# Feed-forward with one 512-column product per weight tile, whole banks, kept hidden units, scaled operands, and another planner clock

## The chip, the cores and the metric

The kernel runs on 1 core of one Trainium2 chip. The metric is the device time of one execution in microseconds (us), median of several runs. The engines of the core are TensorE (PE, matrix products into PSUM; its weight loads are listed apart as PEld), VectorE (DVE), ScalarE (ACT), GpSimd (POOL) and SyncE (SP, which issues most DMAs). PSUM has eight banks; one bank holds 128 partitions x 512 float32.

## The reference

One sequence of 256 tokens, width 1024, goes through a gated recurrent layer, a feed-forward, stick-breaking attention, a second feed-forward, and a second block (a block attention and a chunked recurrence side by side, merged). The change is about the two feed-forwards:

```python
def rms_norm(x, g):
    xf = x.astype(jnp.float32)
    y = xf * lax.rsqrt(jnp.mean(xf * xf, axis=-1, keepdims=True) + RMS_EPS)
    return (y * g.astype(jnp.float32)).astype(x.dtype)

def swiglu_ffn(x, w_in, w_out):          # D_FF = 2816
    gu = jnp.einsum("bsd,df->bsf", x, w_in)
    h = jax.nn.silu(gu[..., :D_FF]) * gu[..., D_FF:]
    return jnp.einsum("bsf,fd->bsd", h, w_out)
...
    h = h + swiglu_ffn(rms_norm(h, ffn_norm[layer]), ffn_w_in[layer], ffn_w_out[layer])
```

## The kernel before, in words

Activations stand with channels on partitions and the 256 tokens as columns; the residual stream is `h`, [128, 8, 256]. All weights, 2128 tiles of 128x128, come in the order of their use in pieces of 8 tiles (`raw`). A float32 product is made of float32r products: `prep` splits each weight into a rounded part `wh` (ACT or DVE, whichever is less behind, `round`) and the rest `wl` (DVE), and `split` does the same to an operand (`hi`, `lo`; tiles xh and xl for a normed `h`, hx for the gated hidden units). `gemm` (L479) multiplies one weight tile by a 256-column operand in three products, wh x hi, wh x lo, wl x hi, into one half `sl` of a bank. `gemm_t` (L491) is the form with the operand standing and 512 weight columns moving.

`Run` writes the program of all engines in one order. It keeps a clock for each engine: `mm` (L275) adds n/2400 + 0.0025 us for a float32r product of n columns to `pe_t`. Work on DVE and ACT that follows a product is a generator (a chain), polled after each weight tile by `tick` and taken a step further when its operands are due by those clocks; `prep_ahead` splits weights ahead, at most `wcap` pieces. `bank` (L296) hands out PSUM banks, four under the tag "acc" and four under "g"; each is a tile [128, 512] of its own, and `free` gives it back. The framework derives the semaphore waits from the reads and writes of tiles.

`ffn` (L982) has 22 pairs of columns j (gate and up, 16 weight tiles each, two halves of one bank). `gu_chain` multiplies the bank by the norm's factor `S` (one 128x512 DVE operation that also empties the bank), applies silu, multiplies, splits into hx. From j = 4 on each j is followed by one K chunk of ff_out (8 weight tiles into four "acc" banks, two outputs m in each); the last `LAST` = 5 chunks come by `project` (L963) and `tail`, bank after bank, and `resid_chain` adds a whole bank to `h`, which starts the next norm.

Other users of the banks, named in the text below by the tile that they fill: z and ge (recurrent layer's projections), ig (its gates, with rg on ACT), qk, vt (attention), fb, qb, aq, ag, bg, ak, gate (second block's projections), mg (merge), ple and o_ (its end), S and v8 (norm rows and a small transposition), ol (attention's output).

Of the kernel before, what the change touches and what calls it, by code (L numbers as in the profile page):

```python
# [11 lines left out]
F32 = mybir.dt.float32  # L12
# [15 lines left out]
# from blocks of this many tokens on, the scores are computed block by block  # L28
# [5 lines left out]
# the order of the recurrent layer's products; 1: in float32, without a split  # L34
# [11 lines left out]
# the order of the second block's projections  # L46
# [113 lines left out]
# the functions that share a table of the scalar engine  # L160
# [15 lines left out]
class Bank:  # L176
    def __init__(self, t, tag):
        self.t, self.tag, self.fresh = t, tag, True
# [5 lines left out]

class Run:
    """Emits the program in one order for all engines. Chains of vector and scalar work are
    generators; each is taken a step further, between matrix products, about when its operands
    are due, so that no engine's queue waits on another's for long."""
# [7 lines left out]
    def __init__(self, nc, tc, ctx, io):  # L196
# [14 lines left out]
        self.bank_live = {"acc": 0, "g": 0}  # L211
        self.bank_free = {"acc": [0.0] * 4, "g": [0.0] * 4}
# [4 lines left out]
    # -- engines, with the time each is thought to be done --  # L217
# [69 lines left out]
    BIG_BUFS = 46  # L287
# [7 lines left out]

    def bank(self, tag):  # L296
        while self.bank_live[tag] >= 4:
            self.advance("bank " + tag)
        self.bank_live[tag] += 1
# [4 lines left out]
        self.n += 1  # L304
        return Bank(self.ps.tile([128, 512], F32, name=f"{tag}_{self.n}", tag=tag, bufs=4), tag)

    def free(self, b, t):
        self.bank_live[b.tag] -= 1
        self.bank_free[b.tag].append(t)

    # -- the chains --
# [5 lines left out]
    def _ready(self, w):  # L317
        if isinstance(w, Fut):
            return self._ready(w.t) if w.t is not None else None
        if isinstance(w, Avail):  # L320
            f = sorted(self.bank_free[w.tag])
            return f[w.n - 1] if len(f) >= w.n else None
# [28 lines left out]
    def advance(self, why):  # L351
        """Nothing to do but to wait for the next step of a chain."""
# [22 lines left out]
    # -- the weights: loaded in the order of their use, split into two parts that sum to them --  # L375
# [54 lines left out]
    def gemm32(self, bank, sl, name, k, m, x, stop):  # L430
        """The same product in float32, which needs no split of the weights."""
# [47 lines left out]
    def gemm(self, bank, sl, name, k, m, x, stop):  # L479
        """One 128 x 128 tile of weights times a [128, 256] operand, to bank[:, sl]."""  # L480
# [9 lines left out]

    def gemm_t(self, banks, name, k, m, x, stop):  # L491
        """The same with the operand standing: tokens by four tiles of outputs."""
# [9 lines left out]
    def round(self, out, a):  # L502
        """To float32r, on the engine that is less behind."""
# [6 lines left out]
    def split(self, src, hi, lo):  # L510
        """hi + lo = src, each exact in float32r; a step of a chain."""
# [5 lines left out]
    # -- reciprocal roots of [128, n] columns, in float32 --  # L517
# [11 lines left out]
    def row(self, out, col):  # L529
        """out[p, t] = col[t, p]: columns of tokens to rows, the columns given for each p."""  # L530
        self.mm(out, col, self.ident, True, True)


def build(r):
# [27 lines left out]
    # ones multiplied until the first data are there: the tensor engine's clock is gated until it has worked  # L562
# [29 lines left out]
    class Norm:  # L592
        def __init__(self, gain, extra=None, first=False):
            """gain: columns; extra: columns of a second gain, with a norm between the two; first: for an
            operand in float32 as well, which is there sooner."""
# [6 lines left out]
            self.hi = [r.big("xh", dt=F32R) for _ in range(2)]  # L602
            self.lo = [r.big("xl", dt=F32R) for _ in range(2)]
            for i in range(8):
                self.x[i].hi = self.hi[i // 4][:, i % 4]
                self.x[i].lo = self.lo[i // 4][:, i % 4]
            for x in self.x:
                x.whole = Fut()

        def pair(self, p, src, dep):  # L610
            """The chain from two chunks of the residual stream to two operands."""
# [88 lines left out]
    def root(out, sums, n, done=None):  # L700
        """One over the root of sums / n + EPS, over [128, 256]."""
# [10 lines left out]
        # a step of Newton's: exp and ln alone leave more than float32's rounding  # L712
# [13 lines left out]
    def tail(banks, name, ks, xs, on_bank, ahead=1):  # L726
        """The last K chunks of a product, bank after bank, so that its results come one after another."""
# [74 lines left out]
    # ================= the recurrent layer =================  # L802
# [160 lines left out]
    def project(name, xs, nk, bias, next_gain, extra=None, accs=None, lead=0, ahead=1):  # L963
        """The rest of a product whose result joins the residual stream, and the norm behind it."""
# [16 lines left out]
    # ================= gated feed-forward =================  # L981
    def ffn(layer, norm, next_gain, extra=None):  # L982
        r.spawn(norm.stats(r.bank("acc"), str(layer) in WIDE))
        hx = [Fut() for _ in range(NJ)]

        def gu_chain(j, bank):
# [8 lines left out]
            o = r.big("hx", [128, 2, 256], F32R)  # L995
            hx[j].hi, hx[j].lo = o[:, 0], o[:, 1]
# [3 lines left out]
        nin, nout = f"ff_in{layer}", f"ff_out{layer}"  # L1000
        bs = [r.bank("g"), r.bank("g")]
# [4 lines left out]
        for j in range(2):  # L1006
            r.spawn(gu_chain(j, bs[j]))
        accs = None
        for j in range(2, NJ):
            b = r.bank("g")  # L1010
            for k in range(8):
                for c in range(2):
                    r.gemm(b, c, nin, k, j + c * NJ, norm.x[k], k == 7)
            r.spawn(gu_chain(j, b))
            kk = j - (LAST - 1)
            if j == 3:
                r.CALM, r.wcap = FFN_CALM, FFN_CAP
            if j == NJ - 1:
                r.CALM, r.wcap = Run.CALM, Run.wcap
            if 0 <= kk < NJ - LAST:  # L1020
                if accs is None:
                    accs = [r.bank("acc") for _ in range(4)]
                for m in range(8):
                    r.gemm(accs[m // 2], m % 2, nout, kk, m, hx[kk], False)
        return project(nout, hx, NJ, None, next_gain, extra, accs, NJ - LAST)

# [679 lines left out]
```

## Time and profile before

| | us |
|---|---|
| median of 3 runs | 838.8 (838.66 to 838.92) |
| span of the profiled execution | 837.3 |
| PE busy in it | 830.4 (99%) |
| DVE busy | 639.1 (76%) |
| ACT busy | 415.6 (50%) |
| feed-forward stages in it, about | 97 to 293 and 390 to 592 |

The profiled execution shows its span from the first to the last instruction; the median of the runs is 1.5 us above that. PE's records overlap, so how far apart products run is read from the starts in its timeline and not from the length of a record. A number in brackets behind a row is the time that the engine stood idle before it and what released it. A group's mean is the length of one record of that shape.

### The profile page before, as it was taken

Reading aid. Unit: us, or ns where it says so; the run is one execution under the profiler, and the core shown is the slowest. Engines: PE = TensorE matmul, PEld = TensorE weight load, DVE = VectorE, ACT = ScalarE, POOL = GpSimd, SP = SyncE. Lnnn points to the kernel's source line nnn. Section 1 sums busy time; section 2 is a strip of 40 time slices with the busy share of each in tenths; the row PEclk is TensorE's granted clock in tenths of the full one; section 3 lists DMA queues with packets and bytes.
Section 4 is the critical chain, followed back from the end, with each engine's and each line's share of the span. In section 5 each row is a group of like instructions: output and inputs, shape, how many; then the busy total and the mean of one; then the engine's idle time right before and its main releaser. Section 6 shows DMA issues by size and latency. Waiting matters only on the chain.

```text
span 837.3 us, 16580 instructions
## 1 busy us (share of the span) xinstructions
PE 830.4 (99%) x6670; PEld 805.8 (96%) x6670; DVE 639.1 (76%) x1236; ACT 415.6 (50%) x821; POOL 24.2 (3%) x57
## 2 busy tenths in 40 slices
PE   8999999999999999999999999999999999999998
PEld 7999999999999998989999999999999899999997
DVE  5999887565665798989976665666799967896774
ACT  4597555454543325364654454543453525645451
POOL 2300000000000001010000000000100000000000
PEclk9999999999999999999999999999999999999999
DMA  8946556655565434455566565664534544546501
GB/s 334 363 138 218 169 188 202 201 183 193 181 203 160 166 93 153 121 168 172 177 202 196 183 200 180 205 194 153 164 101 134 175 146 125 166 138 208 196 26 51
DMA packets 40844, 144.98 MB, mean 173 GB/s; under 512 B 4568, under 2 KB 5616, under 8 KB 40768
## 3 DMA queue, kind: packets, MB, share of 16 engines
q1 hardware_dynamic: 40320, 142.53, 52.7%
q0 software_dynamic: 448, 1.40, 0.6%
q8 instruction: 52, 0.85, 0.4%
q14 instruction: 24, 0.20, 0.1%
HBM read 142.85 MB, written 1.06 MB: 172 GB/s over the span
## 4 chain that ended last, share of the span: by engine, by line
PE 99%; DMA 0%; DVE 0%; issue 0%; ACT 0%; POOLq 0%
PE acc L277 52%; PE g L277 45%; PE g L1099 1%; DMA prm<-in_params 0%; PE g L1437 0%; DVE o L233 0%; DVE qb L233 0%; ACT S L258 0%; ACT o L260 0%; DVE xf L242 0%; POOLq L1663 0%
## 5 line engine op out<-in xcount | busy, mean ns | idle before, releaser
L233 DVE TENSOR_TENSOR wl<-raw,wh 128x512 fp32r<-128x512 f32 x518 | 346.1, 689 | 22.9 <-ACT wh L258 14.4
L277 PE MATMUL g<-xh,wh 128*128 128x256 f32 x808 | 229.9, 284 | 0.0
L277 PE MATMUL g<-xh,wl 128*128 128x256 f32 x808 | 228.6, 283 | 0.0
L277 PE MATMUL g<-xl,wh 128*128 128x256 f32 x808 | 228.6, 283 | 0.0
L258 ACT ACTIVATE wh<-raw 128x512 fp32r<-128x512 f32 x387 | 216.2, 617 | 0.2 <-DMA raw<-in_weights 0.2
L277 PEld LDWEIGHTS g<-xh,wh 128*128 128x128 f32 x808 | 155.1, 192 | 0.8 <-issue 0.6
L277 PEld LDWEIGHTS g<-xl,wh 128*128 128x128 f32 x808 | 155.1, 192 | 0.2
L277 PEld LDWEIGHTS g<-xh,wl 128*128 128x128 f32 x808 | 155.1, 192 | 0.0
L277 PE MATMUL acc<-xh,wh 128*128 128x256 f32 x448 | 129.5, 289 | 0.4 <-DVE qb L233 0.4
L277 PE MATMUL acc<-hx,wh 128*128 128x256 f32 x704 | 128.3, 283 | 0.0
L277 PE MATMUL acc<-xl,wh 128*128 128x256 f32 x448 | 126.6, 283 | 0.0
L277 PE MATMUL acc<-xh,wl 128*128 128x256 f32 x448 | 126.6, 283 | 0.0
L277 PEld LDWEIGHTS acc<-hx,wh 128*128 128x128 f32 x704 | 109.8, 192 | 0.0
L233 DVE TENSOR_TENSOR gu<-g,S 128x512 f32<-128x512 f32 x44 | 30.2, 691 | 95.2 <-PE g L277 95.2
L277 PE MATMUL acc<-hx,wl 128*128 128x256 f32 x352 | 99.6, 283 | 0.0
L260 ACT ACTIVATE gu<-gu 128x256 f32<-128x256 f32 x44 | 18.4, 418 | 160.4 <-DVE gu L233 160.4
L277 PEld LDWEIGHTS acc<-xh,wh 128*128 128x128 f32 x448 | 85.7, 191 | 4.7 <-issue 4.0
L277 PEld LDWEIGHTS acc<-xl,wh 128*128 128x128 f32 x448 | 85.8, 192 | 0.1
L277 PEld LDWEIGHTS acc<-xh,wl 128*128 128x128 f32 x448 | 85.7, 191 | 0.0
L277 PEld LDWEIGHTS acc<-hx,wl 128*128 128x128 f32 x352 | 67.6, 192 | 0.0
L248 DVE CAST wh<-raw 128x512 fp32r<-128x512 f32 x131 | 55.6, 425 | 0.0
L258 ACT ACTIVATE xh<-h,prm 128x256 fp32r<-128x256 f32 x24 | 11.2, 500 | 22.5 <-DVE h L233 13.9
(290 smaller groups left out, 1229.8 us busy)
## 6 DMA issues: line engine op xcount, KB each, us to landing
raw<-in_weights SPq DMA_DIRECT2D x265, 512.0 KB, 3.7
toep<-vrev POOLq DMA_DIRECT2D x2, 512.0 KB, 5.7
h<-in_x SPq DMA_DIRECT2D x1, 512.0 KB, 6.8
raw<-in_weights SPq DMA_DIRECT2D x1, 384.0 KB, 4.4
past<-in_past SPq DMA_DIRECT2D x1, 384.0 KB, 5.5
h<-in_x SPq DMA_DIRECT2D x2, 128.0 KB, 3.4
h<-in_x SPq DMA_DIRECT2D x1, 256.0 KB, 5.3
pt<-in_p POOLq DMA_DIRECT2D x1, 256.0 KB, 5.7
```

Of the source, the lines that this page charges most:

```text
L233: self.nc.vector.tensor_tensor(out, a, b, op)
L248: self.nc.vector.tensor_copy(out, a)
L258: self.nc.scalar.activation(out, a, f, scale=scale, **kw)
L260: self.nc.scalar.activation(out, a, f, bias=bias, scale=scale, **kw)
L277: self.nc.tensor.matmul(out, l, r, start=start, stop=stop, skip_group_check=True)
L1099: nc.tensor.transpose(tb[a].t[:, b], m[:, a, b], r.ident)
```

## The change

The feed-forward's products change form. Operand parts hi and lo lie side by side (tiles xq, hx), and `gemm2` makes one 512-column product wh x [hi | lo] over a whole bank and one 256-column product wl x hi into its first half; the two halves of the bank are added when it is emptied. For ff_in, a column j takes both banks of a PSUM tile (`Pair`): ACT copies the low halves out and DVE adds them to the high halves. `Norm.scaled` makes operands that already hold the factor `S`; columns j whose scaled operands are not there yet by the planner's clock keep the old form (`plain`; j = 0 to 3 in both layers of the built program). ff_out comes after all of ff_in, output m by output m, 22 chunks deep, a bank for each m; `out_chain` adds the two halves to `h` in two DVE operations. All hx stay on chip. PSUM is now four tiles `pp0` to `pp3` of two banks each, handed out by number; that holds for all stages of the kernel. `mm` adds 0.0133 instead of 0.0025 us. `FFN_CAP` goes from 12 to 8. Comments go, too.

```diff
-FFN_CAP = 12
-LAST = 5
+FFN_CAP = 8
...
+class Pair:
+    def __init__(self, t, n):
+        self.n = n
+        self.banks = [Bank(t[:, i], None, 2 * n + i) for i in range(2)]
+        self.high, self.low = t[:, :, 0:256], t[:, :, 256:512]
...
-        self.bank_live = {"acc": 0, "g": 0}
-        self.bank_free = {"acc": [0.0] * 4, "g": [0.0] * 4}
+        self.pp = [self.ps.tile([128, 2, 512], F32, name=f"pp{i}", tag=f"pp{i}", bufs=1) for i in range(4)]
+        self.bank_free = {i: 0.0 for i in range(8)}
...
-            self.pe_t += max(n / 2400, m / 1200) + 0.0025 if l.dtype == F32R else 2 * max(n / 1200, m / 1200) + 0.005
+            self.pe_t += max(n / 2400, m / 1200) + 0.0133 if l.dtype == F32R else 2 * max(n / 1200, m / 1200) + 0.005
...
-    BIG_BUFS = 46
+    BIG_BUFS = 47
...
+    BANKS = {"acc": (0, 1, 2, 3), "g": (4, 5, 6, 7), "any": tuple(range(8))}
+
+    def frees(self, tag):
+        return [i for i in self.BANKS[tag] if i in self.bank_free]
+
     def bank(self, tag):
...
-        self.bank_free[tag].sort()
-        t = self.bank_free[tag].pop(0)
+        n = min(self.frees(tag), key=lambda i: (self.bank_free[i], i))
+        t = self.bank_free.pop(n)
...
-        return Bank(self.ps.tile([128, 512], F32, name=f"{tag}_{self.n}", tag=tag, bufs=4), tag)
+        return Bank(self.pp[n // 2][:, n % 2], tag, n)
+
+    def pair_bank(self):
...
+        n = min(both(), key=lambda i: (when(i), i))
+        self.wait_to(when(n), "pair of banks")
+        del self.bank_free[2 * n], self.bank_free[2 * n + 1]
+        return Pair(self.pp[n], n)
...
+    def gemm2(self, bank, name, k, m, x, stop):
...
+        self.need(x, f"{name} {k}")
+        wh, wl = self.weight(name, k, m)
+        self.mm(bank.t, wh, x.hl, bank.start(), False)
+        self.mm(bank.t[:, 0:256], wl, x.hi, False, stop)
+        self.tick()
...
+        def scaled(self, src):
...
+                    a = r.stt(f[:, c], src[:, 2 * p + c], self.gain[:, 2 * p + c:2 * p + c + 1], self.S, OP.mult, OP.mult)
+                yield a
+                a = yield from r.split(f, t[:, :, 0], t[:, :, 1])
+                self.y[2 * p].t = self.y[2 * p + 1].t = a
...
-            yield norm.s
+            if plain:
+                yield norm.s
             w = r.big("gu")
-            t = r.tt(w[:, 0:2], v2(bank), bc2(norm.S), OP.mult)
-            r.free(bank, t)
+            if plain:
+                t = r.tt(w[:, 0:2], v2(pair), bc2(norm.S), OP.mult)
+            else:
+                yield r.act(w[:, 2:4], pair.low, AF.Copy)
+                t = r.tt(w[:, 0:2], pair.high, w[:, 2:4], OP.add)
+            r.free(pair, t)
...
-            b = r.bank("g")
+            plain = not all(y.t is not None and y.t <= r.pe_t + 0.3 * k for k, y in enumerate(norm.y))
+            b = r.bank("any") if plain else r.pair_bank()
             for k in range(8):
                 for c in range(2):
-                    r.gemm(b, c, nin, k, j + c * NJ, norm.x[k], k == 7)
...
+                    if plain:
+                        r.gemm(b, c, nin, k, j + c * NJ, norm.x[k], k == 7)
+                    else:
+                        r.gemm2(b.banks[c], nin, k, j + c * NJ, norm.y[k], k == 7)
...
-        return project(nout, hx, NJ, None, next_gain, extra, accs, NJ - LAST)
...
+        def out_chain(m, bank):
+            yield r.pe_t + 0.2
+            yield r.tt(h[:, m], bank.t[:, 0:256], h[:, m], OP.add)
+            t = r.tt(h[:, m], bank.t[:, 256:512], h[:, m], OP.add)
+            r.free(bank, t)
+            done[m].t = t
+
+        for m in range(8):
+            b = r.bank("any")
+            for k in range(NJ):
+                r.gemm2(b, nout, k, m, hx[k], k == NJ - 1)
+            r.spawn(out_chain(m, b))
+        return nn
```

How the order of the built program changes, at two places. In the rows a matmul stands as result<-operands with the columns of its result; [waits X] names the engine's semaphore that it waits for.

PE in the end of the second ff_out before: the end of bank acc_681 (outputs 0 and 1), and the start of acc_683's last chunks.

```order
L277 MATMUL acc_682_5212<-hx_900_6976,wl_883_6837 128x256
L277 MATMUL acc_681_5211<-hx_912_7066,wh_887_6870 128x256 [waits DVE_49] x2
L277 MATMUL acc_681_5211<-hx_912_7066,wl_888_6871 128x256
L277 MATMUL acc_681_5211<-hx_912_7066,wh_887_6870 128x256 x2
L277 MATMUL acc_681_5211<-hx_912_7066,wl_888_6871 128x256
L277 MATMUL acc_683_5213<-hx_861_6656,wh_887_6870 128x256 x2
L277 MATMUL acc_683_5213<-hx_861_6656,wl_888_6871 128x256
```

DVE before at that place, where `h_66<-acc_...` is the residual add of a bank:

```order
L233 TENSOR_TENSOR wl_915_7089<-raw_892_6915,wh_914_7088 128x512 [waits DVE_49]
L233 TENSOR_TENSOR h_66<-acc_681_5211,h_66 128x512 [waits PE_49]
L237 SCALAR_TENSOR_TENSOR xl_909_7033<-h_66,der_103,xh_907_7031 128x256 [waits Activation_49] x2
L233 TENSOR_TENSOR h_66<-acc_682_5212,h_66 128x512 [waits PE_49]
L237 SCALAR_TENSOR_TENSOR xl_909_7033<-h_66,der_103,xh_907_7031 128x256 [waits Activation_49] x2
L233 TENSOR_TENSOR h_66<-acc_683_5213,h_66 128x512 [waits PE_49]
```

PE in the first ff_out after: the last chunk of output m = 0 (hx_303, in one bank of pp3) and the first chunks of m = 1 (hx_166, hx_171, hx_183, in the other bank of pp3; the rows name only the tile).

```order
L286 MATMUL pp3_66<-hx_303_2459,wl_310_2477 128x256
L286 MATMUL pp3_66<-hx_166_1455,wh_309_2476 128x512
L286 MATMUL pp3_66<-hx_166_1455,wl_310_2477 128x256
L286 MATMUL pp3_66<-hx_166_1455,wh_309_2476 128x512
L286 MATMUL pp3_66<-hx_166_1455,wl_310_2477 128x256
L286 MATMUL pp3_66<-hx_171_1483,wh_312_2500 128x512 [waits DVE_49]
L286 MATMUL pp3_66<-hx_171_1483,wl_313_2501 128x256
L286 MATMUL pp3_66<-hx_171_1483,wh_312_2500 128x512
L286 MATMUL pp3_66<-hx_171_1483,wl_313_2501 128x256
L286 MATMUL pp3_66<-hx_183_1575,wh_312_2500 128x512 [waits DVE_49]
L286 MATMUL pp3_66<-hx_183_1575,wl_313_2501 128x256
```

DVE after at that place:

```order
L242 TENSOR_TENSOR wl_316_2528<-raw_295_2400,wh_315_2527 128x512 [waits DMAHW5_49,Activation_49]
L242 TENSOR_TENSOR wl_316_2528<-raw_295_2400,wh_315_2527 128x512 [waits Activation_49]
L242 TENSOR_TENSOR h_70<-pp3_66,h_70 128x256 [waits PE_49]
L242 TENSOR_TENSOR wl_319_2551<-raw_299_2431,wh_318_2550 128x512 [waits DMAHW6_49,Activation_49]
L242 TENSOR_TENSOR h_70<-pp3_66,h_70 128x256 [waits DVE_49,PE_49]
L242 TENSOR_TENSOR wl_319_2551<-raw_299_2431,wh_318_2550 128x512 [waits Activation_49]
```

What moved: before, the bank that DVE empties is a tile of its own, and the rows of PE behind it (acc_683) carry no wait. After, the first add `h_70<-pp3_66` waits for the count that the product hx_166 with wl_310 brings, and the product hx_171 with wh_312 for that add; the second add waits for hx_171 with wl_313, and hx_183 with wh_312 for the second add.

The second place is in the second block's projections, the group ag: PE before, from the end of bank acc_1034 to the next bank of the same group.

```order
L277 MATMUL acc_1034_8047<-xh_908_7032,wl_1032_8035 128x256
L277 MATMUL acc_1034_8047<-xh_908_7032,wh_1031_8034 128x256
L277 MATMUL acc_1034_8047<-xl_910_7034,wh_1031_8034 128x256
L277 MATMUL acc_1034_8047<-xh_908_7032,wl_1032_8035 128x256
L277 MATMUL acc_1044_8137<-xh_907_7031,wh_1036_8070 128x256 [waits DVE_49]
L277 MATMUL acc_1044_8137<-xl_909_7033,wh_1036_8070 128x256
L277 MATMUL acc_1044_8137<-xh_907_7031,wl_1037_8071 128x256 [waits DVE_49]
```

DVE before, with the read of that bank, `ag`:

```order
L248 CAST wh_1041_8116<-raw_1021_7951 128x512
L233 TENSOR_TENSOR wl_1042_8117<-raw_1021_7951,wh_1041_8116 128x512 [waits DVE_49]
L237 SCALAR_TENSOR_TENSOR h_66<-h_66,prm_65,S_931_7331 128x256
L233 TENSOR_TENSOR ag_1033_8046<-acc_1034_8047,S_931_7331 128x512 [waits PE_49]
L237 SCALAR_TENSOR_TENSOR h_66<-h_66,prm_65,S_931_7331 128x256
```

PE after at that place (both banks of the group are now in pp0):

```order
L286 MATMUL pp0_63<-xq_700_5634,wh_871_7077 128x256
L286 MATMUL pp0_63<-xq_700_5634,wl_872_7078 128x256 [waits DVE_49]
L286 MATMUL pp0_63<-xq_700_5634,wh_871_7077 128x256 x2
L286 MATMUL pp0_63<-xq_700_5634,wl_872_7078 128x256
L286 MATMUL pp0_63<-xq_700_5634,wh_871_7077 128x256 [waits DVE_49]
L286 MATMUL pp0_63<-xq_700_5634,wh_871_7077 128x256
```

DVE after, with the same read:

```order
L257 CAST wh_877_7143<-raw_863_7015 128x512 [waits DMAHW1_49]
L242 TENSOR_TENSOR wl_878_7144<-raw_863_7015,wh_877_7143 128x512 [waits DVE_49]
L242 TENSOR_TENSOR ag_869_7054<-pp0_63,S_791_6346 128x512 [waits PE_49]
L242 TENSOR_TENSOR wl_878_7144<-raw_863_7015,wh_877_7143 128x512 [waits Activation_49]
L257 CAST wh_880_7173<-raw_866_7037 128x512 [waits DMAHW2_49]
```

What moved: the read of ag itself stands in its queue as before, but the row of PE behind the second weight tile of the next bank (xq_700 with wh_871, the last row but one) now waits for it; before, the rows of acc_1044 wait for their weights alone.

## Rows read from the trace of the kernel before

**Rows 1.** The page: span, busy time by engine, clock in 40 slices, chain by engine.
```profile
span 837.3 us, 16580 instructions
...
PE 830.4 (99%) x6670; PEld 805.8 (96%) x6670; DVE 639.1 (76%) x1236; ACT 415.6 (50%) x821; POOL 24.2 (3%) x57
...
PEclk9999999999999999999999999999999999999999
...
PE 99%; DMA 0%; DVE 0%; issue 0%; ACT 0%; POOLq 0%
```

**Rows 2.** Timeline of PE at 200 us: start us, us, engine line op out<-in xcount.
```profile
200.00 0.28 PE L277 MATMUL g<-xh,wh 128*128 128x256 f32 x1
200.12 0.28 PE L277 MATMUL g<-xl,wh 128*128 128x256 f32 x1
200.24 0.28 PE L277 MATMUL g<-xh,wl 128*128 128x256 f32 x1
200.36 0.28 PE L277 MATMUL g<-xh,wh 128*128 128x256 f32 x1
```

**Rows 3.** Timeline of PE, 744 to 755 us, the stage with the operand standing.
```profile
744.29 0.40 PE L277 MATMUL acc<-wh,xh 128*128 128x512 f32 x1
744.53 0.40 PE L277 MATMUL acc<-wh,xl 128*128 128x512 f32 x1
744.76 0.39 PE L277 MATMUL acc<-wl,xh 128*128 128x512 f32 x1
...
747.04 0.39 PE L277 MATMUL acc<-wh,xh 128*128 128x512 f32 x1
...
754.98 0.39 PE L277 MATMUL acc<-wl,xh 128*128 128x512 f32 x1
```

**Rows 4.** Timeline of all engines at 587 us, end of ff_out.
```profile
587.36 0.28 PE L277 MATMUL acc<-hx,wl 128*128 128x256 f32 x1
...
587.68 0.69 DVE L233 TENSOR_TENSOR h<-acc,h 128x512 f32<-128x512 f32 x1 [1.44 <-PE acc L277]
...
588.08 0.28 PE L277 MATMUL acc<-hx,wl 128*128 128x256 f32 x1
```

**Rows 5.** Timeline of all engines at 612 us, the second block's first products.
```profile
612.77 1.29 DVE L233 TENSOR_TENSOR qb<-acc,S 128x512 f32<-128x512 f32 x2 [1.47 <-ACT S L258]
...
612.89 0.28 PE L277 MATMUL acc<-xh,wl 128*128 128x256 f32 x1
...
613.61 0.36 PE L277 MATMUL acc<-xh,wh 128*128 128x256 f32 x1 [0.44 <-DVE qb L233]
...
613.80 0.28 PE L277 MATMUL acc<-xl,wh 128*128 128x256 f32 x1
```

**Rows 6.** Timeline of all engines at 5 us, the program's first operand.
```profile
5.29 0.35 DVE L242 TENSOR_SCALAR xf<-h,prm 128x256 f32<-128x256 f32 x1 [4.23 <-DMA prm<-in_params]
...
5.71 0.80 PE L277 MATMUL g<-xf,raw 128*128 128x256 f32 x1 [1.25 <-DVE xf L242]
```

**Rows 7.** Groups by line, shapes apart: count | busy, mean ns of one | idle before.
```profile
L233 DVE TENSOR_TENSOR wl<-raw,wh 128x512 fp32r<-128x512 f32 x518 | 346.1, 689 | 22.9 <-ACT wh L258 14.4 <-issue 0.9
...
L233 DVE TENSOR_TENSOR gu<-g,S 128x512 f32<-128x512 f32 x44 | 30.2, 691 | 95.2 <-PE g L277 95.2
...
L237 DVE SCALAR_TENSOR_TENSOR xl<-h,prm,xh 128x256 fp32r<-128x256 f32 x24 | 10.8, 479 | 1.2 <-ACT xh L258 1.2
...
L233 DVE TENSOR_TENSOR h<-acc,h 128x512 f32<-128x512 f32 x12 | 8.3, 690 | 7.7 <-PE acc L277 7.6
...
L233 DVE TENSOR_TENSOR ol<-g,oh 128x256 fp32r<-128x256 f32 x8 | 3.4, 420 | 1.0 <-ACT oh L258 1.0
...
L258 ACT ACTIVATE wh<-raw 128x512 fp32r<-128x512 f32 x387 | 216.2, 617 | 0.2 <-DMA raw<-in_weights 0.2
...
L260 ACT ACTIVATE ig<-acc,prm 128x256 f32<-128x256 f32 x8 | 3.4, 485 | 0.1
...
L258 ACT ACTIVATE ple<-acc 128x512 f32<-128x512 f32 x4 | 2.4, 598 | 2.0 <-PE acc L277 1.9
```

**Rows 8.** Busy time in three windows (core 0: us, PE, PEld, DVE, ACT, POOL).
```profile
200.00:210.00 10.00, 10.00 (x86) 10.00 (x85) 5.63 (x10) 3.94 (x8) 0.00 (x0) 1.00 0.56 186
400.00:410.00 10.00, 10.00 (x84) 9.95 (x83) 9.55 (x19) 5.11 (x12) 0.00 (x0) 1.00 0.58 183
...
620.00:630.00 10.00, 10.00 (x87) 10.00 (x86) 9.96 (x21) 4.48 (x8) 0.00 (x0) 1.00 0.40 119
```

More of the change, by code (lines that the diff above doesn't have):

```diff
@@ L294, in small, with both, when @@
         return self.sb.tile([128, n], F32, name=f"{name}_{self.n}", tag=f"small{n}", bufs=8 if n < 64 else 1)
+    BANKS = {"acc": (0, 1, 2, 3), "g": (4, 5, 6, 7), "any": tuple(range(8))}
+    def frees(self, tag):
+        return [i for i in self.BANKS[tag] if i in self.bank_free]
     def bank(self, tag):
-        while self.bank_live[tag] >= 4:
+        while not self.frees(tag):
             self.advance("bank " + tag)
-        self.bank_live[tag] += 1
-        self.bank_free[tag].sort()
-        t = self.bank_free[tag].pop(0)
+        n = min(self.frees(tag), key=lambda i: (self.bank_free[i], i))
+        t = self.bank_free.pop(n)
         if not self.in_task:
             self.wait_to(t, "bank " + tag)
-        self.n += 1
-        return Bank(self.ps.tile([128, 512], F32, name=f"{tag}_{self.n}", tag=tag, bufs=4), tag)
+        return Bank(self.pp[n // 2][:, n % 2], tag, n)
+    def pair_bank(self):
+        def both():
+            return [i for i in range(4) if 2 * i in self.bank_free and 2 * i + 1 in self.bank_free]
+        def when(i):
+            return max(self.bank_free[2 * i], self.bank_free[2 * i + 1])
+        while not both():
+            self.advance("pair of banks")
+        n = min(both(), key=lambda i: (when(i), i))
+        self.wait_to(when(n), "pair of banks")
+        del self.bank_free[2 * n], self.bank_free[2 * n + 1]
+        return Pair(self.pp[n], n)
     def free(self, b, t):
-        self.bank_live[b.tag] -= 1
-        self.bank_free[b.tag].append(t)
+        if isinstance(b, Pair):
+            self.bank_free[2 * b.n] = self.bank_free[2 * b.n + 1] = t
+        else:
+            self.bank_free[b.n] = t
     in_task = False
@@ L601, in __init__, with parts, chain @@
             self.q = None
[L602 to L606, printed above, removed]
+            self.parts(self.x)
             for x in self.x:
                 x.whole = Fut()
+        def parts(self, x):
+            for p in range(4):
+                t = r.big("xq", [128, 2, 2, 256], F32R)
+                for c in range(2):
+                    f = x[2 * p + c]
+                    f.hl, f.hi, f.lo = t[:, c].rearrange("p a b -> p (a b)"), t[:, c, 0], t[:, c, 1]
+        def scaled(self, src):
+            self.y = [Fut() for _ in range(8)]
+            def chain(p):
+                yield self.s
+                f = r.big("xs", [128, 2, 256])
+                t = r.big("xq", [128, 2, 2, 256], F32R)
+                for c in range(2):
+                    y = self.y[2 * p + c]
+                    y.hl, y.hi, y.lo = t[:, c].rearrange("p a b -> p (a b)"), t[:, c, 0], t[:, c, 1]
+                    a = r.stt(f[:, c], src[:, 2 * p + c], self.gain[:, 2 * p + c:2 * p + c + 1], self.S, OP.mult, OP.mult)
+                yield a
+                a = yield from r.split(f, t[:, :, 0], t[:, :, 1])
+                self.y[2 * p].t = self.y[2 * p + 1].t = a
+            for p in range(4):
+                r.spawn(chain(p))
         def pair(self, p, src, dep):
@@ L1000, in ffn @@
         nin, nout = f"ff_in{layer}", f"ff_out{layer}"
+        r.wcap = FFN_CAP
         bs = [r.bank("g"), r.bank("g")]
@@ L1006, in ffn @@
         for j in range(2):
-            r.spawn(gu_chain(j, bs[j]))
-        accs = None
+            r.spawn(gu_chain(j, bs[j], True))
         for j in range(2, NJ):
-            b = r.bank("g")
+            plain = not all(y.t is not None and y.t <= r.pe_t + 0.3 * k for k, y in enumerate(norm.y))
+            b = r.bank("any") if plain else r.pair_bank()
             for k in range(8):
                 for c in range(2):
-                    r.gemm(b, c, nin, k, j + c * NJ, norm.x[k], k == 7)
[L1014 to L1024, printed above, removed]
-        return project(nout, hx, NJ, None, next_gain, extra, accs, NJ - LAST)
+                    if plain:
+                        r.gemm(b, c, nin, k, j + c * NJ, norm.x[k], k == 7)
+                    else:
+                        r.gemm2(b.banks[c], nin, k, j + c * NJ, norm.y[k], k == 7)
+            r.spawn(gu_chain(j, b, plain))
+            r.CALM = FFN_CALM
+        r.CALM, r.wcap = Run.CALM, Run.wcap
+        nn = Norm(next_gain, extra)
+        done = [Fut() for _ in range(8)]
+        start_norm(nn, h, [done[2 * p:2 * p + 2] for p in range(4)])
+        def out_chain(m, bank):
[10 more added lines that the diff above has]
+        return nn
     norm = ffn(0, norm, pc("mix1", 0, 8))
```

17 lines of the change are left out of this document (11 added, 6 removed).

## The prediction

> **What bounds the kernel now.** I read the page first. PE is busy 830.4 of 837.3 us, 99% of the chain that ended last is PE, and the granted clock is in its top tenth in all 40 slices [rows 1]: the upper level, 2.4 GHz. So the time is the number of products times their spacing, plus what stops PE; work on another engine counts only where PE waits for it. The spacing comes from PE's timeline: three 256-column products take 200.00 to 200.36 [rows 2], 0.120 us each, although a record is 0.28 long (records overlap, so I use starts). A 512-column product shows in the one stage that has the operand standing: from 747.04 to 754.98 there are 35 steps [rows 3], 0.227 each, while the first two after the switch take (744.76 - 744.29) / 2 = 0.235. By windows the feed-forward stages have PE at 10.00 of 10 us and VectorE (DVE) at 5.63 and 9.55, ScalarE (ACT) at 3.94 and 5.11 [rows 8]: nothing to win there but fewer PE cycles.
>
> **What the wide product gives.** One weight tile is three products before, 0.360 us; after, one of 512 columns and one of 256, 0.227 + 0.120 = 0.347. So 13.1 ns a tile (0.2269 unrounded). The built program has 928 tiles in this form: 576 in the two ff_in (18 of the 22 columns j, 16 tiles, 2 layers) and 352 in the two ff_out (8 x 22 x 2). 928 x 13.1 ns = **-12.2 us**, all on the path. By the unsettled 0.235 it would be 928 x 5 ns = -4.6; I take the settled value, since 35 of its steps stand against two, and keep the other for the range.
>
> The Trainium skill, page "TensorE: Matmul & The Clock Gate", section "Back-to-back issue gap", gives N/2.4 + 2.5 ns for one product alone, so 216 ns for 512 columns and 109 for 256. An estimate by that formula is a saving of one 2.5 ns step a tile, 2.3 us in all, and a total 10 us higher than mine; the rows say 227 and 120, so this case's fixed part is near 13 ns and the rows decide.
>
> **What the shared tiles cost.** Before, each bank is a PSUM tile of its own. After, there are four tiles pp0 to pp3 of two banks each, and `bank` takes the bank that was free first, by number between equals; so two products in a row often sit in the two banks of one tile. The waits are kept per tile. The order of the built program shows what that does: the DVE add that reads bank 0 of pp3 (`h_70<-pp3_66`) waits for the last product emitted before it, which writes bank 1, and the next product into bank 1 waits for that add. PE hands over to DVE and waits to get it back, with nothing between. Before, the same read has only its own bank to wait for and PE goes on: the add of 587.68 starts 0.32 after the start (587.36) of the product it waits for, and PE's starts stay 0.12 apart through it up to 588.08 and beyond [rows 4].
>
> Price of one stop, from PE's last start to its next: 0.32 to the reader's start [rows 4]; the reader; then the return to PE; minus the 0.12 that passes anyway. The return has one near row: qb starts at 612.77 and takes 0.69 of its pair's 1.29, so ends near 613.46, and PE, which stood since 612.89 for it, starts at 613.61, 0.15 later, and its next comes at 613.80, 0.07 beyond 0.12 [rows 5]. The lower bound is the first operand of the program, 5.29 + 0.35 = 5.64 to PE at 5.71: 0.07 [rows 6]. I take 0.15 + 0.07, since that is PE waiting in mid-stream for a PSUM reader, as here.
>
> I went through the waits of the built program for those where the product waited for and the product that waits are neighbours on PE:
> - ff_out: after each even m, two adds of 128x256 (0.420 by the row of ol, the same shape out of PSUM) [rows 7]: 0.32 + 0.42 + 0.15 - 0.12 + 0.07 = 0.84. Four m, two adds, two layers: 16 x 0.84 = 13.4 us.
> - A 128x512 read by DVE (0.69, rows gu and h) [rows 7]: 1.11 each. Sixteen: z, ge, one gu in each layer, two qk, fb, ag, bg, ak, four gate, two mg. 17.8 us.
> - Seven others, mostly ACT: v8, S, vt, ple, o_ at about 0.60 (row ple), 1.02 each, 5.1; two ig at 0.485, 0.90 each, 1.8 [rows 7]. 6.9 us.
> - Two more (a qk, aq) with two or three tiles between: 0.4 + 0.2, with the restart 0.7 us.
>
> Together 41 stops, **+38.8 us**. With 0.07 for the return and no restart each is 0.15 less: 32.6. If a reader also came late behind a weight subtraction (0.689, DVE busy about 0.6 of the time: 0.6 x 0.34 x 41), +8.4; taken at 0, since the h reads of before waited for PE and not PE for them [rows 4, 7].
>
> The Trainium skill, page "PSUM — Partial Sum Buffer", section "PSUM bank collisions raise a hardware error", asks for a guard by bank and 32-partition quadrant, with two engines on different banks running clean. The trace agrees: DVE reads one acc bank from 587.68 while PE writes another every 0.12 us. So these waits are not the chip's demand but the program's, and a chip that runs the program keeps them all the same.
>
> **Other parts.** Per layer the scaled operands add 8 operations like xl (0.479) and 4 splits (ACT 0.617 + DVE 0.689, the weights' shape taken); ff_out has 16 adds of 0.420 for 4 of 0.690; 18 pairs get an ACT copy like ple (0.598) while their DVE step stays as long. That is DVE 8 x 0.479 + 4 x 0.689 + 16 x 0.420 - 4 x 0.690 = 10.5 us, ACT 4 x 0.617 + 18 x 0.598 = 13.2, over some 190 us in which DVE is 56 to 96% busy [rows 7, 8]. Cover: weights are split some 16 tiles (5.5 us) ahead of PE, with FFN_CAP at 8 too. Taken at 0; where the cover fails, up to +4. The planner's clock (0.120 for 0.109 us per product) has chains polled after fewer products: real slack per step falls by 9%, some 0.05 us in 0.6. Before shows one stop of this kind, 0.60 us at 612.89 [rows 5]; in the second block's recurrence, where DVE is 9.96 of 10 [rows 8], I bound it at 0 to +2 and take 0. All hidden columns kept (11 big buffers), deep ff_out: no PE work, 0. SP's loads move with the weights, no queue is passed: 0.
>
> **Sum.** Span 837.3 - 12.2 + 38.8 = 863.9; around it lies 838.8 - 837.3 = 1.5 (median against the profiled span). **865.4 us**.
>
> **Rivals.**
> 1. *The stops don't bite*: PE finds each reader done, as at 587.68. Then 838.8 - 12.2 = 826.6, faster. For it: the trace of before, where every evacuation is free. Against: this needs the read to end before the neighbour product is due, and that read can't start until the neighbour before it is done; it decides from a price below 12.2 / 41 = 0.30 us a stop, less than the 0.32 that passes before the reader even starts. 5%.
> 2. *The wide product stays unsettled*, since every second product is of another width and each weight load comes with a product: 0.235, saving 4.6, 873.0. If 512 columns cost what two times 256 do (0.24, as 744.29 to 744.53), saving 0, 877.6. For it: the first steps after a switch [rows 3]; against: nothing says that the switch, and not the phase's start, made them. Inside the forecast's range but for its end; 12%, of which 3% are above the range.
> 3. *Readers late*: DVE comes behind its weight work, 865.4 + 8.4 = 873.8. 10%, of which 2% are above.
> 4. *Cheaper stops*: 865.4 - 6.2 = 859.2; with a fifth of the neighbours drifted apart on the chip, another 7, near 852. 12%, of which 6% are below the range.
>
> **Chances.** The forecast itself, 859 to 872, 59%; rivals 2 to 4 add 34% that are slower too; rival 1 has 5%; some 2% are left for gains and stops that cancel. I call 0.2% (1.7 us) about what a measurement of this kernel can tell from no change. Faster 0.05, same 0.02, slower 0.93. The range goes from 855 (lower stop prices with a few lost) to 877 (nothing saved by the wide product, or late readers with half of it).
>
> **What would show it.** Right: PE's waits list names DVE h some 0.7 to 0.8 us sixteen times, and qk, ag, bg, ak, gate, mg near 1 us; PE's idle time is near 40 us where before it is 6.9; the 512-column starts in ff_in are 0.227 apart from the next; ff_in itself, inside one layer, is 13 ns a tile shorter. Wrong in the saving: steps of 0.235 or 0.24. Wrong in the stops: PE starts 0.12 apart through a read of the other bank of the same tile, or a time under 838. Wrong in the cover: PE waiting for wl or hx in ff_out.

## The result, and the profile after

The changed kernel takes 889.55 us (median of 4 runs, 886.71 to 891.89) against 838.86 for the kernel before, measured beside it: a ratio of 1.0601, 95% interval 1.0583 to 1.0618. Slower was forecast, 865.4 with a range from 855 to 877; the loss is 50.7 us where 26.6 were expected.

The page of the profiled execution, lines that answer to [rows 1]:

```profile
span 890.2 us, 14594 instructions
...
PE 841.1 (94%) x5742; PEld 763.2 (86%) x5742; DVE 698.9 (79%) x1385; ACT 391.1 (44%) x764; POOL 25.6 (3%) x57
...
PEclk9999989999999999999999999999999999899999
...
PE 78%; DVE 14%; ACT 5%; issue 2%; DMA 1%; SPq 0%; ACTq 0%; DVEq 0%
```

PE has 928 products fewer (x5742 for x6670), and still the span is 52.9 us longer. The chain that ended last was 99% PE; now 14% of it is DVE and 5% ACT. And two slices show a clock below the top tenth where before none did. Whom PE waits for, from the list of PE's waits (line waited for: us in total, times, longest us):

```profile
PE pp L286 <- DVE h L242: 8.2, 15, 0.6
PE pp L286 <- DVE gu L242: 7.2, 2, 3.6
PE pp L286 <- DVE gate L242: 6.0, 3, 2.8
PE pp L286 <- DVE qk L242: 2.7, 3, 1.1
...
PE pp L286 <- DVE ag L242: 0.8, 1, 0.8
```

The names are, with a few more (dg, qr, v), those of the prediction; the sizes of gu and gate are not. One stop of ff_out in the timeline, PE and DVE (the answer to [rows 4]):

```profile
240.16 0.28 PE L286 MATMUL pp<-hx,wl 128*128 128x256 f32 x1
...
240.48 0.42 DVE L242 TENSOR_TENSOR h<-pp,h 128x256 f32<-128x256 f32 x1 [2.82 <-PE pp L286]
...
240.96 0.50 PE L286 MATMUL pp<-hx,wh 128*128 128x512 f32 x1 [0.52 <-DVE h L242]
...
241.30 0.28 PE L286 MATMUL pp<-hx,wl 128*128 128x256 f32 x1
...
241.65 0.28 PE L286 MATMUL pp<-hx,wl 128*128 128x256 f32 x1
241.96 0.42 DVE L242 TENSOR_TENSOR h<-pp,h 128x256 f32<-128x256 f32 x1 [0.46 <-PE pp L286]
...
242.44 0.19 PEld L286 LDWEIGHTS pp<-hx,wh 128*128 128x128 f32 x1 [0.83 <-DVE h L242]
```

It takes 0.32 us from PE's start to DVE's, 0.42 for the add and 0.06 back to PE: the round trip as forecast, with the return near its lower bound (0.07). PE's starts lie 0.80 apart, so the gap of a stop costs 0.68. On top of that the first wide product behind the stop takes longer: 240.96 to 241.30 is 0.34, where a wide product's usual step is 0.236 (below), so 0.10 more.

The long stop in the first layer's ff_in, among the first columns j (DVE and PE):

```profile
114.15 3.25 DVE L246 SCALAR_TENSOR_TENSOR xs<-h,prm,S 128x256 f32<-128x256 f32 x8
...
114.86 0.28 PE L286 MATMUL pp<-xq,wl 128*128 128x256 f32 x1
...
117.32 1.28 DVE L242 TENSOR_TENSOR gu<-pp,S 128x512 f32<-128x512 f32 x2
...
118.66 0.80 PE L286 MATMUL pp<-xq,wh 128*128 128x256 f32 x2 [3.52 <-DVE gu L242]
```

The read gu, for which PE waits, stands in DVE's queue behind the eight new xs operations, 3.25 us, and behind another gu read (x2); PE is stopped from 114.86 to 118.66. The long stop of the second layer (PE's starts 438.02 and 441.95) has other work in the queue: the xs operations are done by then, and ahead of gu stand weight subtractions (wl) and the splits of the scaled operands (xq), which are new too. DVE there:

```profile
438.20 0.68 DVE L242 TENSOR_TENSOR xq<-xs,xq 128x512 fp32r<-128x512 f32 x1
...
438.81 0.68 DVE L242 TENSOR_TENSOR wl<-raw,wh 128x512 fp32r<-128x512 f32 x1
439.41 1.28 DVE L242 TENSOR_TENSOR xq<-xs,xq 128x512 fp32r<-128x512 f32 x2
440.61 0.68 DVE L242 TENSOR_TENSOR wl<-raw,wh 128x512 fp32r<-128x512 f32 x1
441.21 0.68 DVE L242 TENSOR_TENSOR gu<-pp,S 128x512 f32<-128x512 f32 x1
```

What the clock does behind the first layer's stop (windows of 2 us: PE, PEld, DVE, ACT, POOL busy, granted clock, DMA):

```profile
116.00:118.00 2.00, 0.00 (x0) 0.00 (x0) 2.00 (x6) 2.00 (x5) 0.00 (x0) 0.77 0.00 0
118.00:120.00 2.00, 1.34 (x6) 1.34 (x7) 2.00 (x5) 1.97 (x4) 0.00 (x0) 0.50 0.00 0
120.00:122.00 2.00, 2.00 (x11) 2.00 (x11) 2.00 (x4) 2.00 (x5) 0.00 (x0) 0.50 0.69 203
124.00:126.00 2.00, 2.00 (x19) 2.00 (x19) 1.52 (x3) 0.42 (x1) 0.00 (x0) 1.00 0.27 109
```

The granted clock is at 0.50, the 1.2 GHz level, while PE works again: 11 products in 2 us where 19 run at 1.00. The same follows the stop at the second layer's gu and that at a gate (PE's starts 766.64 and 769.74). PE works some 5.2, 6.2 and 6.1 us at the lower level, which costs half of that: 8.8 us.

Last, the spacing of the wide product, PE at 170 us (to be read beside [rows 2, 3]). A tile is here the pair of products, one wide and one narrow, for one weight tile:

```profile
169.97 0.40 PE L286 MATMUL pp<-xq,wh 128*128 128x512 f32 x1
170.20 0.28 PE L286 MATMUL pp<-xq,wl 128*128 128x256 f32 x1
170.32 0.40 PE L286 MATMUL pp<-xq,wh 128*128 128x512 f32 x1
170.55 0.28 PE L286 MATMUL pp<-xq,wl 128*128 128x256 f32 x1
170.67 0.40 PE L286 MATMUL pp<-xq,wh 128*128 128x512 f32 x1
```

From 169.97 to 170.67 are two tiles, 0.35 each; over the stage a tile takes 0.3533 us (mean start to start 0.236 for the wide product, 0.117 for the narrow one), not 0.347.

**The account of the 52.9 us of span.** Products: 928 x (0.360 - 0.3533) = -6.2. Steps between PE's starts that exceed the usual spacing by over 0.3 us, their excess summed: 50.7 (that the loss has the same figure is chance), less 2.5 of them before: +48.2. Clock: +8.8. Together 50.8; 2.1 are left. The slower first product behind a stop, 0.10 at each of some 40 stops, is not in these sums and makes some 4 us by itself; so some 2 us went the other way in small steps, and where is not shown. The account is that of the profiled run, the slowest of the four (891.89 us). The mean granted clock of the four is 0.988, 0.992, 0.989 and 0.994, so what the clock costs is not the same in each.

### The profile page after: what moved, and what is told of

Its sections match the earlier page's. It is cut to its first block, busy times and chain, and to the rows that moved or that the text cites. A ratio compares the mean times of both kernels' runs of the same rounds, so it can differ in the third digit from the quotient of the medians.

```text
span 890.2 us, 14594 instructions
## 1 busy us (share of the span) xinstructions
PE 841.1 (94%) x5742; PEld 763.2 (86%) x5742; DVE 698.9 (79%) x1385; ACT 391.1 (44%) x764; POOL 25.6 (3%) x57
## 4 chain that ended last, share of the span: by engine, by line
PE 78%; DVE 14%; ACT 5%; issue 2%; DMA 1%; SPq 0%; ACTq 0%; DVEq 0%
PE pp L286 77%; DVE wl L242 4%; DVE wh L257 1%; ACT wh L267 1%; DVE h L242 1%; DMA h<-in_x 1%; ACT mp L269 1%; ACT L269 1%; PE pp L1182 1%; DVE xs L246 1%; DVE ssq L242 0%; DMA raw<-in_weights 0%; ACT xq L267 0%; PE pp L1520 0%; DVE z L242 0%
## 5 line engine op out<-in xcount | busy, mean ns | idle before, releaser
L286 PE MATMUL pp<-xq,wh 128*128 128x256 f32 (+1 forms) x1936 | 463.2, 324 | 24.8 <-DVE gu L242 7.2
L286 PEld LDWEIGHTS pp<-xq,wh 128*128 128x128 f32 x1936 | 325.9, 194 | 60.6 <-DVE gu L242 7.6
L286 PE MATMUL pp<-xq,wl 128*128 128x256 f32 x1256 | 357.0, 284 | 0.0
L286 PEld LDWEIGHTS pp<-xq,wl 128*128 128x128 f32 x1256 | 242.3, 193 | 0.0
L267 ACT ACTIVATE wh<-raw 128x512 fp32r<-128x512 f32 x284 | 162.7, 618 | 5.6 <-PE pp L286 5.5
L286 PE MATMUL pp<-hx,wh 128*128 128x512 f32 x352 | 126.5, 402 | 8.8 <-DVE h L242 8.2
L257 DVE CAST wh<-raw 128x512 fp32r<-128x512 f32 x234 | 99.1, 423 | 0.0
L286 PE MATMUL pp<-hx,wl 128*128 128x256 f32 x352 | 98.7, 281 | 0.0
L286 PEld LDWEIGHTS pp<-hx,wh 128*128 128x128 f32 x352 | 66.1, 188 | 29.5 <-DVE h L242 8.4
L286 PEld LDWEIGHTS pp<-hx,wl 128*128 128x128 f32 x352 | 66.5, 189 | 0.0
```

The source lines that it names most:

```text
L257: self.nc.vector.tensor_copy(out, a)
L267: self.nc.scalar.activation(out, a, f, scale=scale, **kw)
```

## The experiments

**Each bank a tile of its own.**

```diff
-        self.pp = [self.ps.tile([128, 2, 512], F32, name=f"pp{i}", tag=f"pp{i}", bufs=1) for i in range(4)]
+        self.pp = [self.ps.tile([128, 512], F32, name=f"pp{i}", tag=f"pp{i}", bufs=1) for i in range(8)]
...
-                yield r.act(w[:, 2:4], pair.low, AF.Copy)
-                t = r.tt(w[:, 0:2], pair.high, w[:, 2:4], OP.add)
+                a = [r.act(w[:, 2 + c], pair.banks[c].t[:, 256:512], AF.Copy) for c in range(2)]
+                yield a[1]
+                for c in range(2):
+                    t = r.tt(w[:, c], pair.banks[c].t[:, 0:256], w[:, 2 + c], OP.add)
```

> The changed kernel, but each of the eight PSUM banks is a tile of its own again; a pair's two banks are emptied by two ACT copies of 128x256 and two DVE adds of 128x256 in place of one each over both. Theory (the loss is the waits between neighbours in one shared tile, some with a late reader, plus the clock's falls after the longest three): all of it goes and the wide product's own gain stays, 928 x 6.7 ns = 6.2 us by the spacing read in the trace of after (0.3533 us a tile): 832.6 us, between 831 and 837. Rival (the new shape of the feed-forward, its DVE and ACT work or the deep ff_out, costs the time): it stays above 850.

Measured: 831.66 us, ratio to before 0.9917 (0.9897 to 0.9938). All of PE's waits in its trace:

```profile
PE pp L285 <- DVE xf L250: 2.7, 2, 1.5
PE pp L603 <- DVE der L623: 1.1, 1, 1.1
PE pp L285 <- DVE m L241: 0.6, 1, 0.6
```

xf and der are the start of the program and m is one step of the attention. The clock stays at its upper level, and DVE is 91% busy, more than in any other kernel here, but holds PE up no more than these rows say. So neither the deep ff_out nor the added DVE work makes the loss; without the shared tiles the kernel is 58 us faster, more than the whole loss. The Trainium skill, page "PSUM — Partial Sum Buffer", section "PSUM bank collisions raise a hardware error", asks for a guard by bank and 32-partition quadrant, and calls a guard by bank the simple version of it. This kernel waits by bank, and the trace agrees: DVE's add h of 234.67 to 235.09 reads one bank while PE starts products into another at 234.75 and 234.98, without a stop.

**The wide product taken apart, on own banks.**

```diff
...
-        self.mm(bank.t, wh, x.hl, bank.start(), False)
+        self.mm(bank.t[:, 0:256], wh, x.hi, bank.start(), False)
+        self.mm(bank.t[:, 256:512], wh, x.lo, False, False)
```

> As e1_own_banks, but the 512-column product is made as two of 256 columns, into the two halves of the bank; all else is kept. Theory (in alternation a tile takes 0.3533 us where three narrow products take 0.360): 6.2 us above e1_own_banks, about 838.8. Rival 1, the settled 0.347 of the prediction: 12.2 us above. Rival 2, the wide product gives nothing: equal to e1_own_banks.

Measured: 840.77 us, 9.1 above e1_own_banks, between the two theories. The traces say why. Here all products are 0.120 apart. In e1_own_banks the first layer runs at 0.3467 us a tile and the second at 0.3533:

```profile
169.93 0.39 PE L285 MATMUL pp<-xq,wh 128*128 128x512 f32 x1
170.16 0.28 PE L285 MATMUL pp<-xq,wl 128*128 128x256 f32 x1
170.27 0.39 PE L285 MATMUL pp<-xq,wh 128*128 128x512 f32 x1
170.50 0.28 PE L285 MATMUL pp<-xq,wl 128*128 128x256 f32 x1
170.62 0.39 PE L285 MATMUL pp<-xq,wh 128*128 128x512 f32 x1
...
459.71 0.40 PE L285 MATMUL pp<-xq,wh 128*128 128x512 f32 x1
459.95 0.28 PE L285 MATMUL pp<-xq,wl 128*128 128x256 f32 x1
460.07 0.40 PE L285 MATMUL pp<-xq,wh 128*128 128x512 f32 x1
460.31 0.28 PE L285 MATMUL pp<-xq,wl 128*128 128x256 f32 x1
460.42 0.40 PE L285 MATMUL pp<-xq,wh 128*128 128x512 f32 x1
```

464 x 13.3 ns + 464 x 6.7 ns = 9.3. The same code has two spacings. Here, where PE is not stopped in the feed-forward, a layer keeps one of them from its first wide products to its last; in the kernels with shared tiles it can change at a stop (see the last section).

**The kernel before, with shared tiles and nothing else.** `bank` of the kernel before hands out halves of four two-bank tiles, in its own order.

```diff
...
-        t = self.bank_free[tag].pop(0)
+        t, n = self.bank_free[tag].pop(0)
...
-        return Bank(self.ps.tile([128, 512], F32, name=f"{tag}_{self.n}", tag=tag, bufs=4), tag)
+        return Bank(self.pp[n // 2][:, n % 2], tag, n)
```

> The kernel before, with its banks placed two to a PSUM tile, banks 0 to 3 for the tag acc and 4 to 7 for g; nothing else is changed. Theory (the shared tiles alone make the stops): 25 neighbours in the built program, at 0.94 us each as measured for a 128x512 read in the trace of after, 23.5 us: 862 us, up to 872 where readers come late or the clock falls. Rival (shared tiles are harmless, the feed-forward's new form makes the loss): 838.8 us.

Measured: 901.85 us, ratio 1.0739 (1.0718 to 1.0760), 63 us more, and 2.7 times what counting neighbours gave (23.5). Its steps over 0.3 us sum to 53.7, 51.2 more than before, and the clock falls four times. Much of the excess is late readers in the attention, which the count of neighbours doesn't hold, and at three gates. DVE and PE's weight loads at one of those in the attention:

```profile
352.35 1.75 DVE L1083 TENSOR_TENSOR_SCAN e<-m,past 128x768 f32<-128x768 f32 x1
354.20 1.02 DVE L234 TENSOR_TENSOR m<-pp,e 128x384 f32<-128x384 f32 x2
354.82 0.64 PEld L278 LDWEIGHTS pp<-w,vt 128*64 128x64 f32 x8 [2.60 <-DVE m L234]
```

The reader m waits for a scan of 1.75 us that stands ahead of it; before, PE's list of waits has no m at all. So the shared tiles alone make the loss, without any of the feed-forward's new form.

**ff_out's outputs in other tiles.** First by the planner's choice:

```diff
...
-        n = min(self.frees(tag), key=lambda i: (self.bank_free[i], i))
+        n = min(self.frees(tag), key=lambda i: (i // 2 == last // 2, self.bank_free[i], i))
```

> The changed kernel, but in ff_out each output m takes a bank of another PSUM tile than the output before it. Theory: the 16 stops of 0.67 to 0.77 us at the two ff_out go, 11.0 us; the choice of banks behind them shifts too and has 20 neighbours in place of 24 there: 876 us, between 870 and 882. Rival (ff_out is held by the DVE adds or the operands themselves): 889.

Measured: 890.99 us, no gain, though its two ff_out have no stop at all. Its waits list tells where the time went:

```profile
PE pp L286 <- DVE m L242: 12.3, 6, 2.9
PE pp L286 <- DVE gu L242: 6.6, 2, 3.5
PE pp L286 <- DVE h L242: 3.1, 4, 0.8
```

The shifted choice gave the attention other neighbours, and m, not in the list of the changed kernel at all, costs 12.3 us. TensorE's granted clock, too, fell more often, eight times where it falls three times in the changed kernel: its mean over the profiled run is 0.982, there 0.988. To tell the stop's own price from that, the next one leaves the planner's bookkeeping as it is and only writes each output to another of the same eight banks:

```diff
+PLACES = [[6, 4, 2, 7, 5, 3, 0, 1], [4, 6, 2, 5, 7, 3, 0, 1]]
...
             b = r.bank("any")
+            b.t = r.pp[place[m] // 2][:, place[m] % 2]
```

> The changed kernel with the planner's choice of banks left as it is for every stage, but the eight outputs of each ff_out are written to the same eight banks in another order, so that six of its eight handovers lie in two different tiles. e3_out_other_tile had also moved the banks of the attention and all that follows; this one doesn't. Theory (each stop is paid for itself): 12 of the 16 ff_out stops go, measured in the trace of after at 0.67 to 0.77, together 8.6 us: 881 us, between 879 and 884. Rival (time gained in ff_out is lost again behind it, as e3_out_other_tile may be read): 889.

Measured: 880.89 us (879.68 to 881.15), 8.7 below the changed kernel where 8.6 was expected. So a stop is worth about what its gap in PE's starts shows; nothing gives it back. That the figures meet so closely is in part luck: the 12 stops are 8.8 us of gaps by the two traces and some 1.1 of slower first products behind them, and the profiled spans differ by 12.2 (890.2 and 878.0), since the clock is at 0.50 for 13.7 us here and for 20.5 there.

**The read of gu ahead of the scaled operands.**

```diff
...
-                yield self.s
+                yield [self.s, self.read]
...
             r.free(pair, t)
+            if j == 1:
+                norm.read.t = t
```

> The changed kernel, but in each layer the chains of the scaled operands wait until the banks of j = 0 and 1 have been read, so that on DVE the eight xs operations (3.25 us) stand behind that read and not ahead of it. One column j more takes the old form, 0.1 us. Theory (the stops at gu are 3.7 and 3.8 us because the read is queued behind xs, and the granted clock falls after them): the two stops shrink to 0.94, -5.6 us, and two of the three stretches of 6.8 us at 0.50 go, worth half the time that PE works in them, 2.6 + 3.1 us: 878 us, between 876 and 881. Rival 1 (the clock falls for another reason): -5.6 alone, 884. Rival 2 (the read isn't late by the queue): 889.

Measured: 883.54 us, 6.0 below the changed kernel; neither 878 nor, by its mechanism, 884. In the first layer the stop shrank as expected (PE's starts 114.78 and 115.84, an excess of 0.94) and no fall of the clock follows it. In the second layer the stop is still 2.68 (432.79 to 435.59), since two weight subtractions and a split of the scaled operands stood ahead of that read on DVE, and a fall follows. A new fall comes at 637 us, behind a stop of 1.88 us which the changed kernel has as well, without a fall. In all the clock is at 0.50 for 3.4 us three times, not 6.8 three times. Stops 3.9 less and clock some 3.7 less would make 7.6; the spans differ by 8.2, the medians by 6.0. That a late reader's queue makes the long stops is shown by the first layer; that the falls belong to single stops by their length is not.

**Two tiles together**, wide, wide, narrow, narrow, on own banks:

```diff
...
+        for b, w, x in zip(bs, ws, xs):
+            self.mm(b.t, w[0], x.hl, b.start(), False)
+        for b, w, x, s in zip(bs, ws, xs, stops):
+            self.mm(b.t[:, 0:256], w[1], x.hi, False, s)
```

> e1_own_banks, but two weight tiles are taken together: wide, wide, narrow, narrow in place of wide, narrow, wide, narrow. In e1 a tile takes 0.3467 us in the first layer and 0.3533 in the second. Theory A (each change of width can cost): half of the changes, 0.347 to 0.350 in both layers, 828 to 831. Theory B (the slower spacing is a state that the stream falls into whatever the order): a layer has 0.3467 or 0.3533 here too, 831 to 835. If the two narrow ones behind each other take 0.120 each, as in the kernel before, and the wide ones 0.227: 0.347.

Measured: 832.28 us, ratio 0.9917 (0.9903 to 0.9931), and 0.3483 us a tile in both layers. Mean steps by what follows: wide to wide 0.2329, wide to narrow 0.2333, narrow to narrow 0.1146, narrow to wide 0.1158. So theory B falls for this order, it has one spacing, though the time lies in B's range; but theory A isn't right either, since a wide product behind a wide one costs no less than behind a narrow one. That the smaller spacing doesn't show in the time goes with a second stop for m (1.2 us, 324.72 to 326.18), which e1_own_banks doesn't have. The Trainium skill, page "TensorE: Matmul & The Clock Gate", section "Back-to-back issue gap", has a formula for one product alone; an estimate by it, 216 and 109 ns, is below all of these steps, and the measured steps decide.

**The planner's clock alone**, in the kernel before:

```diff
-            self.pe_t += max(n / 2400, m / 1200) + 0.0025 if l.dtype == F32R else 2 * max(n / 1200, m / 1200) + 0.005
+            self.pe_t += max(n / 2400, m / 1200) + 0.0133 if l.dtype == F32R else 2 * max(n / 1200, m / 1200) + 0.005
```

> The kernel before with the planner's clock alone changed, 0.0133 for 0.0025 us per product. Theory: the chains shift by some products and no wait of weight arises, 838.8 us, up to 2 more in the second block's recurrence. Rival (the clock makes readers late): over 841.

Measured: 841.17 us, ratio 1.0023 (1.0014 to 1.0032): slower by 2.0, the upper end of what was expected (and by the number just over the rival's 841). The place was not the one expected: 1.1 of the 2.0 us arise in the attention, where PE now waits for m once:

```profile
374.81 0.28 PE L277 MATMUL acc<-oh,wl 128*128 128x256 f32 x1
375.67 0.66 PE L277 MATMUL g<-w,vt 128*64 128x256 f32 x4 [0.59 <-DVE m L233]
```

In the second block a stop of 0.48 for hq (627.96 to 628.56) stands in the place of the 0.60 for qb that is gone. The planner's clock also moves work between the engines, since it gives a weight's rounding to the one that is less behind by it: DVE is busy 739.8 us for 639.1, ACT 287.4 for 415.6.

**The old clock on own banks**, with the products in alternation and two by two (each is its base with 0.0025 put back):

> e1_own_banks with the planner's clock put back from 0.0133 to 0.0025 us per product. e7_before_clock showed the new clock to cost the kernel before 2.0 us (0.23%). Theory (the clock costs here what it costs there, and the wide product gains 6 to 12 us whatever the clock): 829.7 us, between 827 and 832. Rival (the new clock fits the new form of the feed-forward): 832 or more.

> e5_two_and_two with the planner's clock put back to 0.0025 us per product. e5 holds 0.3483 us a tile in both layers, where e1_own_banks had 0.3467 in one and 0.3533 in the other. Theory: 832.3 - 2.0 = 830.3 us, and again 0.348 in both layers. Rival (the spacing depends on where the planner puts the other engines' work): another spacing than 0.348.

Measured: 832.51 us (830.24 to 835.62, ratio 0.9921, 0.9900 to 0.9942) in alternation, and 828.90 us (827.94 to 830.05, ratio 0.9877, 0.9864 to 0.9890) two by two. The first lies on the rival's side (832 or more), but it can't tell what the clock is worth: its profiled run has both layers at 0.3533, 3.1 us more than e1_own_banks had, and its runs are spread over 5.4 us, close to the 6.2 between both layers at the one spacing and both at the other. The second has 0.3483 again in both layers and is 3.4 us below e5_two_and_two, where 2.0 was expected. It is faster than both kernels: 10.2 us below before. Its page:

```profile
span 828.3 us, 14656 instructions
...
PE 820.8 (99%) x5758; PEld 755.3 (91%) x5758; DVE 713.6 (86%) x1459; ACT 368.5 (44%) x759; POOL 24.1 (3%) x57
...
PE 99%; DMA 1%; DVE 0%; ACT 0%; issue 0%; ACTq 0%; POOLq 0%
```

## Why the prediction missed, step by step

- **Shared tiles make PE and DVE hand over.** Right, and shown by e1_own_banks (all stops go) and e2_before_shared (they come with the tiles alone). The forecast's sign holds, and so do most of its names.
- **Price of a prompt stop.** Little too high: 0.84 and 1.11 were taken, and the gaps measure 0.67 to 0.77 and 0.94, to which the slower first product behind the stop adds some 0.10. The return took 0.06, near the lower bound of [rows 6], so the 0.15 of [rows 5] was the wrong row to go by for it; the restart, taken at 0.07, is there. For the 16 of ff_out the gaps are 11.4 us, near 13 with the restarts, for 13.4.
- **Readers come promptly.** This is the step that failed most. Eight reads (two gu, three gate, z, fb, vt) were late behind other work on their engine: 19.3 us of stops, against 8.8 in the sum. The prediction priced lateness as an average (rival 3, up to 8.4 spread over all 41) and set it to 0 because the h reads of before were prompt [rows 4, 7]. But a prompt reader is a matter of its queue, and the change itself put new work ahead of gu, eight xs operations in the first layer and splits of the scaled operands in the second: that was one of its own priced edits ("taken at 0"), checked for DVE's total and not for its place.
- **The clock.** Not in the sum: 8.8 us. [rows 5] shows a stop of 0.60 and [rows 1] a clock that never falls; from that nothing was said of stops five times as long.
- **The wide product.** 12.2 us forecast, 6.2 measured. The wide step was 0.236, rival 2's 0.235; its saving of 4.6 came out as 6.2 because the narrow product took 0.117 and not 0.120. On own banks one layer ran at the forecast's 0.3467, but as 0.230 and 0.117, not as 0.227 and 0.120: there the sum of the pair was right by luck, and the wide step of [rows 3] came in no alternation.
- **Other parts at 0.** The planner's clock costs the kernel before 2.0 (e7_before_clock), where 0 to 2 was the bound; but more than half of it arises in the attention and not in the second block's recurrence. What it costs in the changed kernel was not run.

The misses in one line: saving 6.0 short, stops 48.2 for 38.8, clock 8.8 for 0, and the 2.1 that are left make the 26 us between the forecast span of 863.9 and 890.2. The range was too narrow since it let each of these err alone: late readers make long stops, and behind long stops the clock fell.

## What to carry to other kernels

Make the unit of waiting as small as the unit of use: where a framework keeps its waits by tile, one tile per PSUM bank, even if the reader then needs two instructions in place of one. Where a product must wait for a reader, read what stands ahead of that reader in its queue, and price the stop from there and not from the reader's own duration. And test a rearrangement of banks on the whole kernel: e3_out_other_tile removed 16 stops and gained nothing, because the planner dealt others and the clock fell more often.

## What the runs showed of the chip

- A round trip from PE to DVE and back cost 0.32 us to the reader's start, its duration, and 0.06 us back (240.16, 240.48, 240.96), and the first wide product behind it 0.10 more than the others (0.34 from 240.96 to 241.30, for 0.236).
- The same alternation of a 512- and a 256-column product runs at 0.3467 or 0.3533 us a pair, for a whole layer where PE is not stopped. At a stop it can change: in the changed kernel from 0.3533 to 0.3467 at 293.07 us, in e6_gu_first the same way at 254.16 and back at 271.06. What chooses is open. In the order two and two it was 0.3483 in all four layers seen.
- Narrow products among wide ones take 0.115 to 0.117 us, less than the 0.120 they take among their like [rows 2].
- The granted clock fell to 0.50, the 1.2 GHz level, behind stops of 1.88 to 3.82 us (excess over the usual spacing). Every stop of 2.68 us or more that was seen had a fall in it or behind it; of those from 1.88 to 2.61 some did (1.88 in e6_gu_first, 2.27 in e2_before_shared) and some did not (2.02 in the changed kernel, 2.61 in e2_before_shared). What tells them apart was not tried.
